# Two MLPs as one list of block products: weights two steps ahead, weight sums behind the reads of PSUM, first blocks fetched later

## The chip, the cores and the metric

The kernel runs on one core of one Trainium2 chip. The metric is the device time of one execution in microseconds (us). A profiled execution also gives the span from the first to the last instruction and the TensorE clock that was granted, 1.00 being full speed. Engines are named as in the profile: PE (TensorE matmul), PEld (its weight loads), DVE (VectorE), ACT (ScalarE), POOL (GpSimd), SP (the engine that here only issues DMAs).

## The reference

Two layers over 512 tokens of width 1024, all in float32. Layer 0 mixes by gated linear attention, layer 1 by stick-breaking attention; each mixer and each MLP is followed by a layer norm over a scaled residual.

```python
def sq_relu_mlp(x, w_up, w_down):            # x (512, 1024), w_up (1024, 4096), w_down (4096, 1024)
    h = jax.nn.relu(x @ w_up)
    return (h * h) @ w_down

# for each of the two layers
    h = layer_norm(DEEPNORM_ALPHA * h + mix, ln_g[layer, 0], ln_b[layer, 0])
    h = layer_norm(DEEPNORM_ALPHA * h + sq_relu_mlp(h, mlp_w_up[layer], mlp_w_down[layer]),
                   ln_g[layer, 1], ln_b[layer, 1])
```

DEEPNORM_ALPHA is the square root of 2 (`ALPHA` in the kernel). The mixers are not changed, but for the way in which two sums of weights of the layer-0 output projection are formed.

## The kernel before

**A float32 product is three matmuls.** Each float32 operand is cut into `hi` (its value rounded to fp32r) and `lo` (the rest), and a product is hi·hi + hi·lo + lo·hi. For weights, `split_tile` makes `hi` on ACT (L70) and `lo` on DVE (L72), each from a 128x1024 tile; `put` does the same for activations (L98 on ACT, L99 on DVE). Tags "hi" and "lo" have 8 buffers each, so four blocks of weights can stand ready.

**Products are Strassen-Winograd.** A matrix product of 2x2 blocks takes seven block products instead of eight, and sums of blocks before and after. `seven` does that for layer 0's output projection. In `mlp` the 4096 hidden columns are cut into four chunks c of 1024, and each chunk is an *up half* (`up(c)`: x times 1024 columns, 7 products of 48 matmuls of 128x256, L816) and a *down half* (`down(c)`: 1024 hidden values to the 1024 outputs, 7 products of 24 matmuls of 128x512, L909). The halves run as up(0), down(0), up(1), … down(3).

**Weights.** `Blocks` holds the blocks of one half: tag "B" has 8 buffers, four blocks in two tiles (h = 0, 1). The list `AHEAD` gives their order, (0,0), (1,0), (0,1), (1,1). SP loads each tile from HBM (L735). Where the table names a second block, POOL issues a DMA that adds it in flight (L737), so (0,1) becomes (0,1)+(0,0), and (1,1) becomes (1,1)+(0,1). Two further sums are made in place by `onto`: (0,0) += (1,1) and then (1,0) += (0,0), each on two tiles; on DVE (L761), or, for blocks listed in `by`, by a DMA that POOL issues from SBUF to SBUF (L759). The order of the seven products is p(0,0), p(1,0), p(0,1), p(0,0) after its sum, a plain block (1,1) loaded apart, p(1,1), p(1,0) after its sum. The page calls all these tiles B, whatever matrix they hold.

**Reading PSUM.** An up product fills two banks. A *fresh* read copies them on ACT (L824); a *closing* read adds or subtracts them on DVE (L830) and then takes relu and square on ACT (L831, L832); the last product of a half goes from PSUM straight through ACT (L883, L884). A down product is added to the residual rows `h` on DVE (L169, 128x512, or L167 the first time). PSUM has eight banks.

**Order.** The kernel is recorded in program order and a scheduler then places each engine's instructions; each engine runs its list strictly in that order. Instructions under `high_priority` are placed early, those passed through `keep` stay where the program has them. In the lists of before, a half's weight loads, splits and sums stand as early as their buffers allow.

**Start of an MLP.** The four 128-row tiles of `h` are normed one after another: `bn_stats` (L177), `bn_aggr` (L182) on DVE, `ve` and `rs` (L183, L184) on POOL, centring on DVE (L190), eight transposes per tile on PE (L261). Tiles 0 and 1 are turned before the first up product; those of tiles 2 and 3 are interleaved with the first two products (list `late`), from matmul step n = 8 of the first and n = 4 of the second. up(0) works on columns already split apart (`pieces_512`, or `ready` in layer 1). Its `Blocks` has `by` = (0,0), (1,0): four L759 DMAs in POOL's queue. The affine part of the norm (L196, per tile a product and a sum of two halves each) is done beside up(0) and down(0); the factor ALPHA of the residual sits in the first add (L167).

**End of an MLP.** down(3) has `by` = (0,0), (1,0) in both layers, so that all four sums are L759 DMAs. Its last three products are interleaved with the next norm.

## Time and profile before

| what | value |
| --- | --- |
| median of 3 runs | 1216.42 us (1211.41 to 1217.33) |
| the profiled execution | 1221.53 us |
| its span | 1219.8 us |
| mean granted TensorE clock | 0.949 |
| busy in that span | PE 1113.7, PEld 963.8, DVE 895.8, ACT 672.1, POOL 187.5 us |
| idle time of PE within the two MLPs and their starts | 18 gaps, 99.7 us |
| MLP of layer 0 | first up product's end of transposes 252.8 to 602.7 us |
| MLP of layer 1 | 864.5 to 1209.4 us |

The profiled execution is 5.11 us above the median and 1.73 us longer than its span. PE is busy 91% of the span, but a matmul at half clock counts as busy for twice as long, so the busy time holds the price of a low clock too. In a row of a timeline, a bracket at the end gives the idle time just before and what ended it. In a row of a table of windows stand the stretch, its length, then busy time and count for PE, PEld, DVE, ACT and POOL, the granted clock, the share of time for which the DMA engines were busy, and GB/s.

### The profile page before, as it was taken

The numbers are of one execution on the slowest core, as the hardware profiler recorded it, in microseconds if no ns is written. First come the engines' busy times: TensorE is split into PE (matmuls) and PEld (weight loads), VectorE is DVE, ScalarE is ACT, GpSimd is POOL, SyncE is SP. The second block draws the span as 40 slices with busy tenths as digits, with TensorE's granted clock in tenths as the row PEclk, the third lists the DMA queues.
The fourth block names the chain that finished last, engine by engine and source line by source line (L and its number), as shares of the span: only waits on it lengthen the run. The fifth ranks groups of instructions, "written<-read, shape, count | busy, mean of one in ns | idle before, by whom it ended". The sixth has DMA issues, their size and how long they took to land. (4 is left out here: it accounts for less than half of the span.)

```text
span 1219.8 us, 16750 instructions
## 1 busy us (share of the span) xinstructions
PE 1113.7 (91%) x6463; PEld 963.8 (79%) x6463; DVE 895.8 (73%) x1095; ACT 672.1 (55%) x963; POOL 187.5 (15%) x217
## 2 busy tenths in 40 slices
PE   9999998599978978998899999996999979979977
PEld 7888886597877877896788677785888868968965
DVE  4587467589758758686987887685898677677857
ACT  4464353585465455465674667755764644644743
POOL 1011220410110110111204001212021101101111
PEclk9999999799998998998999899997899979989989
DMA  7153696968866676677756216559478667667673
GB/s 218 53 172 87 187 237 150 245 184 188 223 166 176 145 191 174 151 195 170 211 114 191 88 63 128 121 148 232 141 190 211 182 164 183 178 171 170 198 182 69
DMA packets 125187, 202.77 MB, mean 166 GB/s; under 512 B 14202, under 2 KB 39162, under 8 KB 125108
## 3 DMA queue, kind: packets, MB, share of 16 engines
q1 hardware_dynamic: 92756, 131.97, 34.2%
q0 software_dynamic: 29888, 65.02, 29.7%
q10 hardware_dynamic: 2464, 4.72, 1.2%
q8 instruction: 51, 0.84, 0.3%
q14 instruction: 28, 0.23, 0.1%
HBM read 181.76 MB, written 3.15 MB: 152 GB/s over the span
## 5 line engine op out<-in xcount | busy, mean ns | idle before, releaser
L70 ACT ACTIVATE hi<-B 128x1024 fp32r<-128x1024 f32 x206 | 216.7, 1058 | 198.6 <-PE ps L909 38.9
L72 DVE TENSOR_TENSOR lo<-B,hi 128x1024 fp32r<-128x1024 f32 x206 | 247.6, 1221 | 87.8 <-ACT hi L70 87.6
L909 PE MATMUL ps<-hi,T 128*128 128x512 f32 x896 | 285.2, 398 | 15.7 <-ACT T L98 15.6
L816 PE MATMUL ps<-T,hi 128*128 128x256 f32 x1280 | 246.4, 295 | 45.8 <-DVE s L830 41.6
L816 PEld LDWEIGHTS ps<-T,hi 128*128 128x128 f32 x1280 | 211.3, 203 | 49.8 <-DVE s L830 43.4
L909 PEld LDWEIGHTS ps<-hi,T 128*128 128x128 f32 x896 | 171.4, 192 | 55.1 <-ACT T L98 17.3
L816 PE MATMUL ps<-T,lo 128*128 128x256 f32 x640 | 185.5, 293 | 0.0
L909 PE MATMUL ps<-lo,T 128*128 128x512 f32 x448 | 177.7, 398 | 0.0
L816 PEld LDWEIGHTS ps<-T,lo 128*128 128x128 f32 x640 | 129.0, 203 | 0.1
L70 ACT ACTIVATE hi<-raw 128x1024 fp32r<-128x1024 f32 x88 | 92.2, 1057 | 59.5 <-PE ps L94 15.0
L72 DVE TENSOR_TENSOR lo<-raw,hi 128x1024 fp32r<-128x1024 f32 x86 | 104.0, 1217 | 24.4 <-ACT hi L70 24.2
L909 PEld LDWEIGHTS ps<-lo,T 128*128 128x128 f32 x448 | 86.1, 192 | 17.8
L761 DVE TENSOR_TENSOR B<-B,B 128x1024 f32<-128x1024 f32 x36 | 43.2, 1222 | 77.2 <-DMA B<-in_mlp_w_down_dram 44.3
L816 PE MATMUL ps<-A,hi 128*128 128x256 f32 x512 | 93.0, 284 | 0.8 <-ACT s L824 0.6
L816 PEld LDWEIGHTS ps<-A,hi 128*128 128x128 f32 x512 | 79.8, 192 | 1.4 <-ACT s L824 1.4
L93 PE MATMUL ps<-T,hi 128*128 128x512 f32 (+1 forms) x200 | 80.1, 401 | 0.0
L737 POOL DMA_DIRECT2D B<-in_mlp_w_down_dram x32 | 38.7, 1210 | 258.5 <-DVE lo L72 189.8
L95 PE MATMUL ps<-T,lo 128*128 128x512 f32 (+1 forms) x200 | 76.6, 383 | 0.0
L94 PE MATMUL ps<-T,hi 128*128 128x512 f32 (+1 forms) x200 | 76.5, 382 | 0.0
L169 DVE TENSOR_TENSOR h<-h,ps 128x512 f32<-128x512 f32 x108 | 72.4, 680 | 2.2 <-PE ps L1254 1.5
L737 POOL DMA_DIRECT2D B<-in_mlp_w_up_dram x32 | 38.8, 1228 | 225.1 <-DMA B<-in_mlp_w_up_dram 136.8
L816 PE MATMUL ps<-A,lo 128*128 128x256 f32 x256 | 72.4, 283 | 0.0
(229 smaller groups left out, 1925.2 us busy)
## 6 DMA issues: line engine op xcount, KB each, us to landing
B<-in_mlp_w_up_dram SPq DMA_DIRECT2D x64, 512.0 KB, 4.4
B<-in_mlp_w_down_dram SPq DMA_DIRECT2D x64, 512.0 KB, 4.7
B<-in_mlp_w_up_dram POOLq DMA_DIRECT2D x32, 512.0 KB, 9.3
B<-in_mlp_w_down_dram POOLq DMA_DIRECT2D x32, 512.0 KB, 9.6
B<-B POOLq DMA_DIRECT2D x28, 512.0 KB, 5.2
raw<-in_mlp_w_up_dram SPq DMA_DIRECT2D x24, 512.0 KB, 4.9
raw<-in_gla_w_in_dram SPq DMA_DIRECT2D x20, 512.0 KB, 3.9
raw<-in_mlp_w_down_dram SPq DMA_DIRECT2D x16, 512.0 KB, 8.6
```

Source lines behind the costliest of these rows:

```text
L70: keep(nc.scalar.activation(hi, raw, AF.Copy))
L72: keep((on or nc.vector).tensor_tensor(lo, raw, hi.bitcast(F32), op=ALU.subtract))
L93: keep(nc.tensor.matmul(ps, lhsT=a[0], rhs=b[0], start=first, stop=False))
L94: keep(nc.tensor.matmul(ps, lhsT=a[0], rhs=b[1], start=False, stop=False))
L95: keep(nc.tensor.matmul(ps, lhsT=a[1], rhs=b[0], start=False, stop=last))
L169: nc.vector.tensor_tensor(h, h, ps, op=op)
L737: nc.gpsimd.dma_start(out=b.rearrange("p (a b) -> p a b", a=2), in_=weights(other[0], h, other[1]), accum_op=ALU.add)
L761: tt(x, x, y, op=ALU.add)
L816: nc.tensor.matmul(to, lhsT=b[k][x][:, fs], rhs=a(k)[:, y], start=opens and f % 2 == 0 and (k, x, y) == (0, 0, LO), stop=closes and (k, x) ...
L909: nc.tensor.matmul(banks[s], lhsT=a(k)[:, x][:, P * s:P * s + P], rhs=b[k][y], start=opens and (k, x, y) == (0, LO, 0), stop=closes and (k ...
```

## The change

1. **Steps.** up and down no longer run product by product: every block product becomes a `Step` with three parts, its weights (`blocks`), its activations (`operand`) and its matmuls and reads (`go`). All 56 steps of an MLP stand in one list `todo`, and `run_all` walks it: when it comes to step n it makes the weights of step n + 2 (and, from n = 6 on, that step's operand) and then issues step n.
2. **Sums behind.** `onto` now takes one half h, forms the sum and splits it at once, all four instructions held in program order by `keep`. It is called as the `blocks` of the two steps that use the sums, so two steps ahead and no earlier. DVE sums have line L767, DMA sums L765.
3. **Start.** up(0) keeps only (1,0) in `by`. Its `Blocks` loads (0,1) and (1,1) through SP as before; (0,0) and (1,0), four tiles, are loaded by POOL (L876) behind a copy of the last tile's `rs` (`pin`, L932). The late transposes in the first product move from n = 8 to m = 13 of its 16 places.
4. **Affine.** L196 is cut in two: `times` (a 128x1024 product, L199) beside up(0) and down(0), and `plus` (L202, with ALPHA) beside up(1).
5. **Output projection of layer 0.** `ends` is gone from `seven`: the sums of (1,1) and (2,1) blocks were formed by ten accumulating DMAs from HBM (L342) and are now four DMAs from SBUF to SBUF (L351).
6. One list of differences in the stick-breaking layer passes through `keep`.

```diff
-    def seven(a1, a2, weights, pool, hs, fresh, norms=(), mid=None, ends=False, begun=None):
+    def seven(a1, a2, weights, pool, hs, fresh, norms=(), mid=None, begun=None):
...
+        def onto(b, a):
+            nc.gpsimd.dma_start(out=b, in_=a, accum_op=ALU.add)
...
-            if ends:
-                more(b11, h, 0, 1)
-                more(b11, h, 1, 1)
-            else:
-                tt(b11, b22, b11, op=ALU.add)
+            onto(b11, b22)
...
-        def onto(self, a, b):
-            for x, y in zip(self.b[a], self.b[b]):
-                if a in self.by:
-                    nc.gpsimd.dma_start(out=x, in_=y, accum_op=ALU.add)
-                else:
-                    tt(x, x, y, op=ALU.add)
+        def onto(self, a, b, h):
+            x, y = self.b[a][h], self.b[b][h]
+            if a in self.by:
+                keep(nc.gpsimd.dma_start(out=x, in_=y, accum_op=ALU.add))
+            else:
+                keep(tt(x, x, y, op=ALU.add))
+            hi, lo = split_tile(x, 2, keep)
+            return [(hi[:, i, :], lo[:, i, :]) for i in range(2)]
...
+            table = (
+                (ys, True, False, (0, 0), True, blocks(0, 0, True)),
+                (xs, True, True, (0, 0), False, blocks(1, 0, True)),
+                (zs, True, False, (1, 1), True, blocks(0, 1)),
+                (ys, False, False, (0, 1), True, blocks(0, 0, sums=((0, 0), (1, 1)))),
+                (zs, False, True, (0, 1), False, blocks(2, 2)),
+                (ys, False, False, (1, 1), False, blocks(1, 1)),
+                (ys, False, True, (1, 0), None, blocks(1, 0, sums=((1, 0), (0, 0)))),
+            )
...
+                if after and n == 0:
+                    me.rest = lambda: (after(), made[0].load(AHEAD[:2], lambda **to: keep(nc.gpsimd.dma_start(**to))))
...
-                bs = Blocks(mlp_, w, AHEAD[2:] + AHEAD[:2], ((0, 0), (1, 0)))
...
+                    if c == 0 and late and (n == 0 and m == 13 and len(late) > 1 or n == 1 and m == 4):
+                        late.pop(0)()
...
+                def after():
+
+                    nc.gpsimd.tensor_copy(out=small(1, "pin"), in_=last)
+
+                made = steps(r[0], r[2], r[1], r[3], w, part, read, AHEAD[2:], ((1, 0),), plain, ops, after)
...
+        def run_all():
+            for n, step in enumerate(todo):
+                if n == len(todo) - 7:
+                    yield
+                for m in range(n, n + 3) if n == 0 else (n + 2,) if n > 5 else ():
+                    if m < len(todo):
+                        todo[m].make_blocks()
+                        if m > 6 or m < 2:
+                            todo[m].make_operand()
+
+                def between():
+                    if n == 0:
+                        step.rest()
+                    if n == 1:
+                        todo[2].make_operand()
+                    if 0 < n <= 5:
+                        todo[n + 2].make_operand()
+                        todo[n + 2].make_blocks()
+
+                yield from step.go(between)
```

Three places where the lists of instructions differ follow. B, lo, hi are weight tiles and their splits, ps a PSUM bank, s the up half's result, T an activation operand; numbers tell buffers apart and differ between the two programs.

The first is DVE at the passage from up(1) to down(1) in layer 0. Before, the sums of down(1)'s blocks (L761) stand ahead of up(1)'s closing reads of product 6 (L830, `ps516` and `ps517`):

```order
L830 TENSOR_TENSOR s2515_2915<-s2515_2915,ps529_3041 128x2x256
L761 TENSOR_TENSOR B548_3336<-B548_3336,B554_3350 128x1024
L72 TENSOR_TENSOR lo560_3365<-B549_3338,hi559_3363 128x1024
L761 TENSOR_TENSOR B549_3338<-B549_3338,B555_3353 128x1024
L830 TENSOR_TENSOR s2515_2915<-s2515_2915,ps516_2916 128x2x256
L99 TENSOR_TENSOR T563_3395<-s2515_2915,T563_3395 128x4x256
L830 TENSOR_TENSOR s2515_2915<-s2515_2915,ps517_2917 128x2x256
L72 TENSOR_TENSOR lo565_3400<-B550_3340,hi564_3398 128x1024
L72 TENSOR_TENSOR lo567_3404<-B551_3342,hi566_3402 128x1024
```

After, those reads carry line L915, and the first sum (L767) stands behind them and behind the first two adds of down(1) (L169):

```order
L915 TENSOR_TENSOR s2526_2965<-s2526_2965,ps523_2914 128x2x256
L72 TENSOR_TENSOR lo563_3305<-B551_3224,hi562_3303 128x1024
L915 TENSOR_TENSOR s2526_2965<-s2526_2965,ps524_2915 128x2x256
L72 TENSOR_TENSOR lo565_3309<-B552_3226,hi564_3307 128x1024
L99 TENSOR_TENSOR T566_3311<-s2526_2965,T566_3311 128x4x256
L72 TENSOR_TENSOR lo568_3368<-B553_3228,hi567_3366 128x1024
L72 TENSOR_TENSOR lo570_3372<-B554_3231,hi569_3370 128x1024
L830 TENSOR_TENSOR tmp571_3374<-s2526_2965,s2525_2964 128x1024
L169 TENSOR_TENSOR h304_1638<-h304_1638,ps573_3379 128x512
L99 TENSOR_TENSOR T572_3376<-tmp571_3374,T572_3376 128x4x256
L169 TENSOR_TENSOR h305_1639<-h305_1639,ps574_3393 128x512
L767 TENSOR_TENSOR B549_3220<-B549_3220,B555_3234 128x1024
```

So a wait of the sum for its transfers came ahead of reads that PE's last up product waits for, and now it comes behind them; the second sum of that block stands four rows further down.

The second is POOL at the start of layer 0's MLP. Before, the norms of tiles 2 and 3 (L183, L184) alternate with the sums by DMA (L759), each of which waits for transfers:

```order
L737 DMA B402_2082<-in_mlp_w_up_dram 128x2x512
L737 DMA B403_2085<-in_mlp_w_up_dram 128x2x512
L759 DMA B404_2088<-B402_2082 128x1024
L759 DMA B405_2090<-B403_2085 128x1024
L183 TENSOR_SCALAR ve382_2020<-mv381_2019 128x1
L184 TENSOR_TENSOR rs383_2021<-ve382_2020,mhalf_73 128x1
L759 DMA B406_2092<-B404_2088 128x1024
L759 DMA B407_2094<-B405_2090 128x1024
L183 TENSOR_SCALAR ve385_2041<-mv384_2040 128x1
L184 TENSOR_TENSOR rs386_2042<-ve385_2041,mhalf_73 128x1
```

After, they stand directly behind the loads, and the pinned copy and the plain loads come behind the last norm:

```order
L743 DMA B402_2076<-in_mlp_w_up_dram 128x2x512
L743 DMA B403_2079<-in_mlp_w_up_dram 128x2x512
L183 TENSOR_SCALAR ve382_2014<-mv381_2013 128x1
L184 TENSOR_TENSOR rs383_2015<-ve382_2014,mhalf_73 128x1
L183 TENSOR_SCALAR ve385_2035<-mv384_2034 128x1
L184 TENSOR_TENSOR rs386_2036<-ve385_2035,mhalf_73 128x1
L932 COPY pin412_2158<-rs386_2036 128x1
L876 DMA B413_2160<-in_mlp_w_up_dram 128x2x512
L876 DMA B414_2162<-in_mlp_w_up_dram 128x2x512
L876 DMA B415_2164<-in_mlp_w_up_dram 128x2x512
L876 DMA B416_2166<-in_mlp_w_up_dram 128x2x512
L765 DMA B415_2164<-B413_2160 128x1024
```

All four sums have left the norms' neighbourhood; two of them (L767) are now DVE's, the others (L765) come later in POOL's list.

The third is ACT at the passage into down(3) of layer 1. Before, the splits of the summed tiles (`hi785<-B752`, `hi787<-B753`) stand between the final reads of the up half and the operand `T777`:

```order
L70 ACTIVATE hi785_4993<-B752_4842 128x1024
L883 ACTIVATE s2710_4410<-ps712_4412 128x2x256
L884 ACTIVATE s2710_4410<-s2710_4410 128x2x256
L70 ACTIVATE hi787_4997<-B753_4844 128x1024
L883 ACTIVATE s2710_4410<-ps713_4413 128x2x256
L884 ACTIVATE s2710_4410<-s2710_4410 128x2x256
L98 ACTIVATE T777_4946<-tmp776_4944 128x4x256
```

After, the final reads come first, then the operand `T776`, then the splits of the first summed tiles (`B745`, `B746`):

```order
L912 ACTIVATE s2721_4464<-ps719_4414 128x2x256
L913 ACTIVATE s2721_4464<-s2721_4464 128x2x256
L912 ACTIVATE s2721_4464<-ps720_4415 128x2x256
L913 ACTIVATE s2721_4464<-s2721_4464 128x2x256
L98 ACTIVATE T776_4882<-tmp775_4880 128x4x256
L70 ACTIVATE hi779_4914<-B745_4716 128x1024
L70 ACTIVATE hi781_4919<-B746_4718 128x1024
```

The wait of a split for a sum by DMA came ahead of the last reads of the up half and of `T777`; now it comes behind both.

More of the change, by code (lines that the diff above doesn't have):

```diff
@@ L838, in other @@
+                if also and n >= (4 if c == 0 else 1):
                     also.pop(0)()
-            if c == 0:
-                ops[0], ops[1] = views([hT.a[0]]), views([hT.a[1]])
-            product(ops[0], p1, ys, True, False, (lambda n: n == 8 and len(late) > 1 and late.pop(0)()) if c == 0 else None)
-            fresh(ys, 0, 0)
+                return ()
+            r = [lambda u=u, s=s: hT.r[u][:, :, s] for u in range(2) for s in (LO, HI)]
             if c:
-                p2 = bs.pieces(1, 0)
@@ L885, in up @@
-            return a1, a2
-        def down(c, a1, a2, norms=(), by=(), also=()):
+                made = steps(*(None,) * 4, w, part, read, AHEAD, ops=ops)
+            else:
+                plain = [ready[:4], ready[4:]] if ready else [pieces_512(mlp_w_up[l], 512 * k, 4, 0) for k in range(2)]
+                last = hs[3].rs
+                def after():
+                    nc.gpsimd.tensor_copy(out=small(1, "pin"), in_=last)
+                made = steps(r[0], r[2], r[1], r[3], w, part, read, AHEAD[2:], ((1, 0),), plain, ops, after)
@@ L888, in down @@
+            return made, [lambda s=s, j=j: sq[j][:, :, s] for j in range(2) for s in (LO, HI)]
+        def down(c, q, norms=(), by=(), also=()):
             w = lambda k, h, j: block(mlp_w_down[l], 1024 * c + 512 * k + 256 * h, 512 * j)
-            a11, a21, a12, a22 = a1[:, :, LO], a1[:, :, HI], a2[:, :, LO], a2[:, :, HI]
-            bs = Blocks(mlp_, w, AHEAD, by)
-            ys, xs, zs = ([None, None] for _ in range(3))
             seen = set()
             also = list(also)
-            def other():
-                if also:
-                    also.pop(0)()
@@ L913, in product @@
-            def product(a, b, banks, opens, closes, i, j, last=False):
-                for s in range(2):
-                    part(s, a, b, banks, opens, closes)
-                    add(s, banks, i, j, last)
-            first = operand(a11)
-            product(first, bs.pieces(0, 0), ys, True, False, 0, 0)
-            second = operand(a12), bs.pieces(1, 0)
-            other()
-            product(*second, xs, True, True, 0, 0, last=True)
-            t = temp()
-            tt(t, a22, a21, op=ALU.subtract)
@@ L925, in down @@
-            third = operand(t), bs.pieces(0, 1)
-            other()
-            bs.onto((0, 0), (1, 1))
-            product(*third, zs, True, False, 1, 1)
-            minus(t, t, a11)
-            bs.onto((1, 0), (0, 0))
-            fourth = operand(t), bs.pieces(0, 0)
-            product(*fourth, ys, False, False, 0, 1)
-            minus(a12, a12, t)
-            p3 = operand(a12), bs.plain(1, 1)
-            tt(a11, a11, a21, op=ALU.subtract)
-            p7 = operand(a11), bs.pieces(1, 1)
@@ L951, in mlp, with part @@
-        keep = tc.keep_in_program_order
-        turns = [lambda h=h: h.affine(vec, keep) for h in hs]
-        for c in range(NC - 1):
-            a1, a2 = up(c, turns[:2] if c == 0 else ())
-            for _ in down(c, a1, a2, by=((1, 0),), also=turns[2:] if c == 0 else ()):
-                pass
-        a1, a2 = up(NC - 1)
-        steps = down(NC - 1, a1, a2, norms=range(NT) if l == 0 else (2, 3), by=((0, 0), (1, 0)))
-        got = done(steps, four, mlp_)
+            def part(a, b, banks, opens, closes, n):
+                for s in range(2):
+                    if opens:
+                        banks[s] = bank()
+                    for k in range(4):
+                        for x, y in ((LO, 0), (LO, 1), (HI, 0)):
+                            nc.tensor.matmul(banks[s], lhsT=a(k)[:, x][:, P * s:P * s + P], rhs=b[k][y],
+                                             start=opens and (k, x, y) == (0, LO, 0),
+                                             stop=closes and (k, x) == (3, HI), skip_group_check=True)
+                    yield s
@@ new lines, in read @@
+            def read(s, banks, i, j, first, n):
+                last = not first and 2 * i + s in norms
+                hs[2 * i + s].add(j, banks[s], c == 0 and (i, j, s) not in seen, last, ALU.subtract if j else ALU.add)
+                seen.add((i, j, s))
+                if also and s == 1 and n < 2:
+                    also.pop(0)()
+                if norms and n > 3:
+                    yield (s, ~s, 2 + s)[n - 4]
+            return steps(q[0], q[2], q[1], q[3], w, part, read, AHEAD, by)
@@ L960, in mlp @@
+        every = run_all()
+        next(every)
+        got = done(every, four, mlp_)
         ml.__exit__(None, None, None)
@@ L1313, in yoco_kernel @@
             if p == 1:
-                differences(1)()
+                differences(1)(keep)
         if p == NP - 1:
```

203 lines of the change are left out of this document (100 added, 103 removed).

## The prediction, made before the changed kernel was run

> **What bounds the kernel now.** I read the page first, then PE's and DVE's waits, then windows laid around PE's long gaps, and last the timelines at these places. From the page, engine totals and one group:
>
> ```profile
> PE 1113.7 (91%) x6463; PEld 963.8 (79%) x6463; DVE 895.8 (73%) x1095; ACT 672.1 (55%) x963; POOL 187.5 (15%) x217
> L761 DVE TENSOR_TENSOR B<-B,B 128x1024 f32<-128x1024 f32 x36 | 43.2, 1222 | 77.2 <-DMA B<-in_mlp_w_down_dram 44.3
> ```
>
> PE is the bound by its average, but no engine is full. The DVE sums cost 43.2 us of work and 77.2 us of waiting ahead of them. The waits of PE (us in total, times, longest), then those of DVE and POOL:
>
> ```profile
> PE ps L816 <- DVE s L830: 41.6, 4, 11.0
> PE ps L261 <- DVE h L190: 21.4, 5, 10.5
> PE ps L909 <- ACT T L98: 15.6, 4, 6.6
> PE ps L261 <- DVE mv L182: 11.5, 2, 8.1
> DVE B L761 <- DMA B<-in_mlp_w_down_dram: 44.3, 8, 11.6
> DVE h L190 <- POOL rs L184: 27.8, 12, 11.8
> ```
>
> Four waits of PE for a closing read (L830) make 41.6 us, and eight waits of DVE for down weights make 44.3. One of the four shows that they are the same thing. DVE first, then PE, after up(1) of layer 0:
>
> ```profile
> 352.92 1.28 DVE L830 TENSOR_TENSOR s<-s,ps 128x512 f32<-128x512 f32 x2
> 365.36 1.23 DVE L761 TENSOR_TENSOR B<-B,B 128x1024 f32<-128x1024 f32 x1 [11.16 <-DMA B<-in_mlp_w_down_dram]
> 367.90 1.23 DVE L761 TENSOR_TENSOR B<-B,B 128x1024 f32<-128x1024 f32 x1 [0.18 <-DMA B<-in_mlp_w_down_dram]
> 369.04 0.68 DVE L830 TENSOR_TENSOR s<-s,ps 128x512 f32<-128x512 f32 x1
> 369.78 0.58 PE L816 MATMUL ps<-T,hi 128*128 128x256 f32 x1 [10.74 <-DVE s L830]
> ```
>
> The read that PE needs stands behind two sums of weights for the next half, which wait until 365.36 and 367.90 for their transfers. What this costs per half is read from windows that end where PE's products of a half end. The first, third, fourth and fifth are the four up halves with the stall, the second is a down half and the sixth an up half without one, the seventh is down(3) of layer 1, the eighth and ninth are the two starts, and the last is 3.4 us after a short gap:
>
> ```profile
> 324.85:378.23 53.38, 42.45 (x330) 42.04 (x329) 31.82 (x31) 27.34 (x31) 7.85 (x7) 0.87 0.69 161
> 378.23:416.33 38.10, 38.10 (x170) 31.53 (x169) 32.52 (x34) 21.09 (x22) 4.83 (x4) 1.00 0.78 210
> 416.33:470.47 54.14, 43.10 (x337) 42.90 (x336) 31.89 (x31) 26.35 (x30) 6.61 (x6) 0.87 0.63 144
> 939.14:992.64 53.50, 42.42 (x329) 42.01 (x328) 31.83 (x31) 27.31 (x31) 7.81 (x7) 0.87 0.69 162
> 1030.75:1082.15 51.40, 42.56 (x337) 42.35 (x336) 31.89 (x31) 26.64 (x30) 7.02 (x7) 0.90 0.63 149
> 1120.26:1160.94 40.68, 40.68 (x338) 40.48 (x337) 29.44 (x29) 25.61 (x29) 5.85 (x5) 1.00 0.70 185
> 1160.94:1207.49 46.55, 39.90 (x162) 31.57 (x161) 31.39 (x38) 21.39 (x27) 4.92 (x7) 0.89 0.44 107
> 207.70:252.82 45.12, 25.13 (x157) 23.31 (x157) 27.48 (x38) 25.68 (x50) 12.72 (x16) 0.81 0.89 219
> 829.25:864.48 35.23, 22.15 (x135) 20.49 (x135) 20.23 (x26) 20.61 (x40) 8.15 (x11) 0.80 0.84 228
> 300.60:304.00 3.40, 3.40 (x10) 2.58 (x9) 3.40 (x4) 2.66 (x4) 0.00 (x0) 0.50 1.00 217
> ```
>
> A quiet up half takes 40.68 us and a quiet down half 38.10, both with PE busy throughout at clock 1.00. Those are the floors.
>
> **The change, part by part.**
>
> *A. Sums behind the closing reads.* The excess of the four stalled halves is 53.38 + 54.14 + 53.50 + 51.40 − 4 × 40.68 = 49.7 us. Idle time and the half clock that follows it are both in that. In the new order the reads come ahead of the sums, so this wait goes. What is late next is the sum itself. Before, its two transfers had landed 40.5 and 43.1 us after the half began (365.36 and 367.90 against 324.85). The new places are behind the first two adds of the down half, about 40.7 + 5.4 (a seventh of 38.10) = 46.1 us, and some 4 us further down. Buffers come free a few microseconds later too, since the sums and splits that read them move back, so the slack is between 0 and about 6 us. I keep 2 us per half, 1 of idle time and 1 of clock, and take 49.7 − 8 = 41.7. The bounds are 0 (the stall keeps its size under another name) and 49.7.
>
> DVE is the cover, and it is thin in a down half. By the order, a down half after the change has 14 `lo` splits, 2 sums, 7 operand splits and 4 differences, 27 instructions of 128x1024, and 14 adds of 128x512. Back to back they take what the chain shows in down(3):
>
> ```profile
> 1187.07 1.14 DVE T L99
> 1188.21 0.59 DVE h L169
> ```
>
> 27 × 1.14 + 14 × 0.59 = 39.0 us against 38.10 of PE. Over a pair of halves the sum is what DVE does now, 31.82 + 32.52 = 64.3 us in 40.68 + 38.10 = 78.8. The excess of 0.9 fits in the two steps of lead (2 × 5.4 us), which the up half rebuilds, so I cost it at nothing. Without that lead it is 6 × 0.9 = 5.4 us.
>
> *B. Splits behind the last reads in down(3).* PE waited there on an operand that stood behind the split of a summed tile. ACT, PE, and the two sums in POOL's queue, layer 1:
>
> ```profile
> 1173.79 1.06 ACT L70 ACTIVATE hi<-B 128x1024 fp32r<-128x1024 f32 x1 [11.10 <-DMA B<-B]
> 1178.39 0.79 PE L909 MATMUL ps<-hi,T 128*128 128x512 f32 x1 [6.61 <-ACT T L98]
> 1163.92 0.90 POOL L759 DMA_DIRECT2D B<-B  x1 [4.68 <-DMA B<-in_mlp_w_down_dram]
> 1166.51 0.86 POOL L759 DMA_DIRECT2D B<-B  x1 [1.69 <-DMA out_dram<-lnb]
> ```
>
> This half's excess is 46.55 − 38.10 = 8.45 us. Layer 0 has the smaller one. L909's four waits are 15.6 in all: 6.61 here, 2.14 and 1.86 at the two down(0) (E below), which leaves 4.99, and by proportion 4.99 × 8.45 / 6.61 = 6.4 us of excess. After the change the operand goes first, and the split is wanted only by the fourth product, 3 × 5.44 = 16.3 us into the half. The second sum was issued 5.6 us into it and, at the first one's 9.8 us (1163.92 to about 1173.7), lands at 15.4. With buffers free 3 to 4 us later it is about 3 us late in layer 1, 5 with the clock. In layer 0 I keep 1. Saved: 3.4 + 5.4, rounded down to 8.4. Bounds 0 and 14.8.
>
> *C. Start of layer 0's MLP.* Two waits of PE, the POOL and DVE rows behind the second:
>
> ```profile
> 215.77 1.52 PE L261 MATMUL ps<-ident,h 128*128 128x128 f32 x6 [8.07 <-DVE mv L182]
> 238.44 1.97 PE L261 MATMUL ps<-ident,h 128*128 128x128 f32 x8 [10.51 <-DVE h L190]
> 233.42 0.90 POOL L759 DMA_DIRECT2D B<-B  x1 [12.78 <-DMA B<-in_mlp_w_up_dram]
> 235.73 0.86 POOL L759 DMA_DIRECT2D B<-B  x1 [1.42 <-DMA B<-in_mlp_w_up_dram]
> 207.59 1.06 ACT L70 ACTIVATE hi<-B 128x1024 fp32r<-128x1024 f32 x1 [12.44 <-DMA B<-in_gla_w_o_dram]
> ```
>
> The norm of tile 2 stood in POOL's queue behind two sums that waited for transfers, and its L190 behind that. The new order has L183 and L184 ahead of every sum, so 10.51 goes. The other wait, 8.07, is for statistics that stand on DVE behind the split of output-projection weights whose DMA sum landed at 207.5. These ten accumulations from HBM become four from SBUF, issued for the same tiles; medians on the page:
>
> ```profile
> B<-in_mlp_w_down_dram POOLq DMA_DIRECT2D x32, 512.0 KB, 9.6
> B<-B POOLq DMA_DIRECT2D x28, 512.0 KB, 5.2
> ```
>
> Up to three accumulations in a row at 9.6 become one at 5.2, so this wait goes too. In full clock the stretch holds 25.13 × 0.81 = 20.4 us of PE work; with 3.1 for an operand gap of E's size below and its clock it lasts 23.5 and saves 21.6. Against that, two sums that POOL did (L759) are now DVE's, with their splits, ahead of the third product's reads: 4 × 1.14 = 4.6 us if nothing covers them, 0 if all is covered; I take 3.1 (and 1 of clock), because up(0) has little DVE slack while it also splits its own operands. Net 17.5; bounds 0 and 24.7.
>
> The four plain loads cross to POOL's queue and wait there for the last `rs`. Four issues at L759's 0.90 and a landing like its 5.2 end some 9 us after that norm; the sums that use them are formed two products later (2 × 40.68 / 7 = 11.6 us), so I cost them at nothing; uncovered, they cost one landing, 5.2 us. The pinned copy and the transposes' later place cost what a POOL row of 0.6 and 16 small matmuls cost anyway: 0.
>
> The Trainium skill ("DMA: Bandwidth & Descriptors", section "SWDGE vs HWDGE vs iDMA") speaks against this move: plain transfers belong on SP or ACT, and GpSimd is for accumulation. If that price falls on the path in both layers, the sum is 2 × 5.2 us worse, 1153; the rows above put it behind cover, and I go by them.
>
> *D. Start of layer 1's MLP.* The same reordering, with less to win:
>
> ```profile
> 834.58 0.90 POOL L759 DMA_DIRECT2D B<-B  x1 [0.82 <-DMA B<-in_mlp_w_up_dram]
> 837.33 0.90 PE L261 MATMUL ps<-ident,h 128*128 128x128 f32 x3 [8.08 <-DVE h L190]
> ```
>
> L759 goes, but POOL still issues its accumulations behind SP's loads ahead of this norm. L759's part is 0.82 + 0.90 = 1.7 ahead of this tile and as much ahead of the next, each with 1.7 of clock (E): 6.8 in all, less 3.1 as in C and rounded down: 3.5. Bounds −3 and 17.5 (35.23 − 22.15 × 0.80).
>
> *E. down(0) and the affine.* The first products of down(0) in the two layers:
>
> ```profile
> 300.23 0.93 PE L909 MATMUL ps<-hi,T 128*128 128x512 f32 x2 [2.14 <-ACT T L98]
> 914.29 0.74 PE L909 MATMUL ps<-hi,T 128*128 128x512 f32 x2 [1.86 <-ACT T L98]
> ```
>
> PE waits there beside L196's rows, half of which move to up(1). Each such gap also had a half-clock stretch of 3.40 us behind it (last window), so 1.7 more: 7.4 in both layers. I take 2; bounds −2 and 7.4.
>
> On that clock the Trainium skill ("TensorE: Matmul & The Clock Gate", Part 1) has the throttle return after an idle window of about 3.4 us and asks only for no gap above that. Here a gap of 2.14 us was followed by 3.40 us at 0.50, so the trace differs and I charge clock to short gaps. By the page the leftover gaps would cost no clock, and the sum would be about 6 us better, 1137.
>
> **The sum.** 41.7 + 8.4 + 17.5 + 3.5 + 2 = 73.1. The profiled 1221.53 becomes 1148.4; it stood 5.1 above the median of 1216.42, so against that median I expect 1143.
>
> **Rivals.**
>
> *R1, the transfers become the bound.* The same bytes move in less time. A pair of halves moved with share 0.69 × 53.38 + 0.78 × 38.10 = 66.5 us of full DMA time; in 78.8 that is 0.84, and up to 0.89 and 1.00 are seen in the windows above. If the last accumulated blocks are then late in each of the six pairs by 3 us with 1.7 of clock, it is 28 us: 1171. For it: the slack of 0 to 6 us in A. Against it: the share stays below 0.89.
>
> *R2, everything closes.* All upper bounds, 49.7 + 14.8 + 24.7 + 6.7 + 7.4 = 103.3, give 1113. Against it: the slack of DVE and of the sums.
>
> *R3, slower.* Splits for step n + 2 stand on DVE and ACT ahead of the reads of earlier steps; one tile that is late then holds the queue at each step, where before it held one product per pair. It decides at 73 / 56 = 1.3 us per product in all 56 of them; at 1.8 the time is 1244. For it: 39.0 against 38.1 in down halves. Against it: in the quiet halves the same splits stand as far ahead, with no gap.
>
> *R4, the stall only changes its name.* The sum's wait meets the adds of the down half and A saves nothing: 1143 + 41.7 = 1185. Against it: transfers that land at 43.1 for a place at 46.1.
>
> **How the numbers follow.** Forecast 0.73, R1 0.12, R2 0.06, R4 0.04, R3 0.03, no net change 0.02. The forecast's own range is 1125 to 1163. From R2's upper part to R1's and the start of R4's, 1117 to 1178 leaves out about 0.18. About 0.5% (6 us) can be told from no change: faster 0.94, same 0.02, slower 0.04 (R3 and a part of the unforeseen).
>
> **What would show it.** A: the up halves c = 1, 2 at 41 to 43 us, clock 1.00, no wait of PE for a closing read above 2 us; the sums' line waits less than 20 us in all. B: down(3) below 44 us. C: 207.70 to the end of the last transposes near 27, no L190 wait for POOL above 3 us. D: 32. The prediction is wrong if PE waits on weights (`hi`, `lo`) at the third or seventh step of each half (R1), on adds (R4), or if small gaps stand at most steps (R3).

## The result, and the profile after

The median is 1130.13 us (1128.15 to 1137.22) against 1216.88: ratio 0.931 (0.926 to 0.936), 86.8 us faster. The profiled execution took 1129.37 us with a span of 1127.6. The forecast of 1143 was 13 us too slow, within its range. Between the two profiled executions the spans differ by 92.2 us, because the one before stood 5.1 us above its median and the one after 0.8 us below.

Engine totals, the granted clock in 40 slices, and the group of DVE sums after the change, from the page (the group from the view by lines):

```profile
PE 1091.5 (97%) x6463; PEld 942.9 (84%) x6463; DVE 898.9 (80%) x1083; ACT 669.8 (59%) x963; POOL 182.8 (16%) x217
PEclk9999999999999999999999999998999999999989
L767 DVE TENSOR_TENSOR B<-B,B 128x1024 f32<-128x1024 f32 x40 | 48.8, 1219 | 1.0 <-DMA B<-in_mlp_w_up_dram 1.0
```

PE's idle time in the whole span fell by 70.0 us, from 106.1 to 36.1. (Within the two MLPs and their starts the 18 gaps of before add up to 94.1 us, not 99.7.) PE has the same 6463 matmuls, but 22 us less busy time, since fewer of them ran at half clock. The sums are four more than before, 40 for 36, and DVE waits 1.0 us ahead of them where it waited 77.2. The longest waits of PE, in the same columns as those of before:

```profile
PE ps L948 <- ACT T L98: 8.1, 4, 3.5
PE ps L267 <- DVE h L190: 8.0, 3, 5.8
PE ps L899 <- DVE lo L72: 3.7, 4, 1.5
PE ps L948 <- DVE h L169: 2.1, 1, 2.1
```

The wait of 41.6 us for closing reads is gone, that for statistics (11.5) too, and the other two of before are 8 us each. Where the time came from shows in windows whose bounds are the same points of the program in both kernels: the end of the output projection's uninterrupted products, of down(0), of down(2), of down(3), and the same in layer 1. Before:

```profile
207.70:325.01 117.31, 95.19 (x572) 85.41 (x573) 97.90 (x116) 70.29 (x99) 22.97 (x25) 0.91 0.79 199
325.01:508.74 183.73, 161.77 (x1003) 148.03 (x1002) 128.61 (x130) 95.89 (x103) 22.90 (x20) 0.93 0.70 175
508.74:602.69 93.95, 85.07 (x522) 75.94 (x521) 70.31 (x78) 55.04 (x72) 14.46 (x15) 0.95 0.72 174
602.69:829.25 226.56, 223.94 (x1260) 177.99 (x1259) 178.32 (x260) 143.40 (x273) 37.03 (x47) 0.98 0.52 132
829.25:939.31 110.06, 95.06 (x550) 84.99 (x551) 90.66 (x104) 64.36 (x89) 18.41 (x20) 0.89 0.72 189
939.31:1120.42 181.11, 161.19 (x1002) 147.46 (x1002) 128.60 (x130) 96.15 (x103) 23.22 (x21) 0.93 0.71 178
1120.42:1209.36 88.94, 82.29 (x505) 73.42 (x505) 62.66 (x69) 48.08 (x56) 11.17 (x12) 0.94 0.56 141
```

After:

```profile
207.67:307.20 99.53, 94.07 (x588) 83.02 (x589) 88.20 (x97) 67.12 (x96) 23.28 (x27) 1.00 0.87 221
307.20:463.50 156.30, 156.30 (x1001) 142.65 (x1001) 133.24 (x135) 94.45 (x102) 23.07 (x21) 1.00 0.79 203
463.50:550.96 87.46, 82.91 (x507) 73.83 (x506) 66.78 (x75) 50.84 (x68) 13.14 (x16) 0.96 0.71 174
550.96:771.53 220.57, 219.74 (x1260) 176.29 (x1259) 181.36 (x262) 146.62 (x277) 36.27 (x46) 1.00 0.55 138
771.53:873.82 102.29, 91.41 (x566) 81.32 (x567) 88.22 (x95) 65.39 (x90) 19.97 (x23) 0.97 0.77 202
873.82:1031.22 157.40, 156.65 (x1001) 142.68 (x1001) 133.14 (x135) 94.34 (x102) 23.51 (x21) 1.00 0.79 202
1031.22:1118.58 87.36, 81.71 (x491) 72.68 (x490) 63.90 (x70) 48.05 (x56) 13.06 (x14) 0.94 0.56 143
```

In the two middle pairs of each layer PE is now busy throughout at clock 1.00, but for one wait of 0.74 us in layer 1. After the change more matmuls of the next up half stand ahead of the last product of a down half than before: 16 more at the end of down(0), which are 1.9 us, and 15 more at the end of down(2), 1.8 us. Moved back to their own stage, the savings against the terms forecast are:

| stage | saved, us | forecast |
| --- | --- | --- |
| chunks 1 and 2 (A) | 27.4 + 23.7 − 2 × (1.9 − 1.8) = 50.9 | 41.7 |
| chunk 3 (B) | 6.5 + 1.6 − 2 × 1.8 = 4.5 | 8.4 |
| start and chunk 0, layer 0 (C, half of E) | 17.8 + 1.9 = 19.7 | 18.5 |
| start and chunk 0, layer 1 (D, half of E) | 7.8 + 1.9 = 9.7 | 4.5 |
| between the MLPs | 6.0 | 0 |
| after the last product | 1.4 | 0 |

Together they are 92.2, the difference of the spans (1219.8 − 1127.6).

### The profile page after: what moved, and what is told of

Same layout as the page of the kernel before. It is cut to its first block, busy times and chain, and to the rows that moved or that the text cites. A ratio compares the mean times of both kernels' runs of the same rounds, so it can differ in the third digit from the quotient of the medians.

```text
span 1127.6 us, 16741 instructions
## 1 busy us (share of the span) xinstructions
PE 1091.5 (97%) x6463; PEld 942.9 (84%) x6463; DVE 898.9 (80%) x1083; ACT 669.8 (59%) x963; POOL 182.8 (16%) x217
## 5 line engine op out<-in xcount | busy, mean ns | idle before, releaser
L70 ACT ACTIVATE hi<-B 128x1024 fp32r<-128x1024 f32 x206 | 213.5, 1054 | 158.5 <-DVE B L767 65.6
L948 PE MATMUL ps<-hi,T 128*128 128x512 f32 x896 | 286.4, 397 | 11.5 <-ACT T L98 8.1
L899 PE MATMUL ps<-T,hi 128*128 128x256 f32 x1280 | 233.0, 284 | 4.4 <-DVE T L99 2.0
L948 PEld LDWEIGHTS ps<-hi,T 128*128 128x128 f32 x896 | 170.7, 191 | 52.6 <-ACT T L98 10.2
L899 PEld LDWEIGHTS ps<-T,hi 128*128 128x128 f32 x1280 | 199.5, 192 | 8.2 <-ACT T L98 2.7
L899 PE MATMUL ps<-T,lo 128*128 128x256 f32 x640 | 179.7, 284 | 3.7 <-DVE lo L72 3.7
L899 PEld LDWEIGHTS ps<-T,lo 128*128 128x128 f32 x640 | 121.9, 192 | 5.0 <-DVE lo L72 4.8
L948 PEld LDWEIGHTS ps<-lo,T 128*128 128x128 f32 x448 | 85.7, 191 | 17.8 <-DVE lo L72 0.7
L98 ACT ACTIVATE T<-s 128x1024 fp32r<-128x1024 f32 (+1 forms) x52 | 51.5, 993 | 53.2 <-DVE s L842 37.0
L169 DVE TENSOR_TENSOR h<-h,ps 128x512 f32<-128x512 f32 x108 | 71.4, 680 | 4.2 <-PE ps L948 3.5
```

Source lines behind the costliest of these rows:

```text
L70: keep(nc.scalar.activation(hi, raw, AF.Copy))
L98: keep(nc.scalar.activation(hi, ps, AF.Copy))
L169: nc.vector.tensor_tensor(h, h, ps, op=op)
L899: nc.tensor.matmul(to, lhsT=b[k][x][:, fs], rhs=a(k)[:, y], start=opens and f % 2 == 0 and (k, x, y) == (0, 0, LO), stop=closes and (k, x) ...
L948: nc.tensor.matmul(banks[s], lhsT=a(k)[:, x][:, P * s:P * s + P], rhs=b[k][y], start=opens and (k, x, y) == (0, LO, 0), stop=closes and (k ...
```

## The experiments

The kernel after was timed in one group of runs, with the median of 1130.13 us above, while the kernel before was timed in every group and had medians between 1216.42 and 1220.3. So a difference of about 3 us or less against 1130 says little by itself.

**The sums alone, in the kernel before.**

```diff
-                    tt(x, x, y, op=ALU.add)
+                    tc.keep_in_program_order(tt(x, x, y, op=ALU.add))
```

> The kernel before with one change: the DVE sums of weights (L761) are held in program order, so that in the lists they stand behind the closing reads of the up half and beside the first adds of the down half, as after the change; steps, lead, start, affine and output projection stay as before. Theory 1 (the place of the sums behind the reads is the whole of A): the four stalled up halves fall from 51.4 to 54.1 us to 41 to 42, about 48 us come off, near 1168 us. Rival (the lead of two steps and the splits made with the sums are needed as well): the wait moves into the down halves, less than 25 us come off, above 1190 us.

Measured: 1166.29 us against 1217.56 for the kernel before, ratio 0.957 (0.955 to 0.960), 51 us. Chunks 1 and 2 of both layers:

```profile
327.26:487.44 160.18, 157.42 (x1002) 142.97 (x1002) 129.12 (x132) 94.43 (x103) 22.86 (x20) 1.00 0.79 200
908.56:1065.80 157.24, 156.84 (x1002) 142.80 (x1002) 129.06 (x132) 94.41 (x103) 22.85 (x20) 1.00 0.80 204
```

They take 160.2 and 157.2 us where they took 183.7 and 181.1; with the same bounds they take 156.4 and 157.5 after the change. One word on one line, and with it the place of 36 instructions in DVE's list, is 47.4 of A's 50.9 us. The 3.5 us that are left sit in layer 0.

**The sums not held, in the kernel after.**

```diff
-                keep(tt(x, x, y, op=ALU.add))
-            hi, lo = split_tile(x, 2, keep)
+                tt(x, x, y, op=ALU.add)
+            hi, lo = split_tile(x, 2)
```

> The kernel after with keep taken off the DVE sum and its split, the program's order unchanged. In the lists the sums then stand behind the last closing reads but ahead of the first add of the down half, about 5 us earlier than after the change. Theory 1 (what counts is that the closing reads come first): pairs of halves stay within 2 us of after, 1130 to 1136. Rival R4 (a wait of the sums for their transfers just meets the next reads, the adds): 4 pairs with 3 to 6 us more, 1142 to 1154.

Measured: 1200.79 us (1196.37 to 1207.61). R4 was too small: 71 us go. Chunks 1 and 2 take 184.0 and 186.1 us in the two layers, 56 more together, and the first chunks 14 more. The edit did not do what the expectation took for granted, that the sums stay behind the closing reads. In down(2) of both layers a sum stands ahead of such a read (L915) again, as in the kernel before. Layer 0:

```profile
443.43 1.23 DVE L767 TENSOR_TENSOR B<-B,B 128x1024 f32<-128x1024 f32 x1 [6.34 <-DMA B<-in_mlp_w_down_dram]
448.22 0.68 DVE L915 TENSOR_TENSOR s<-s,ps 128x512 f32<-128x512 f32 x1
448.95 0.79 PE L899 MATMUL ps<-T,hi 128*128 128x256 f32 x2 [6.83 <-DVE s L915]
```

The sums for up(2) and up(3) stand ahead of an add of the down half before. Layer 0, and the matmul that waits for that add:

```profile
400.17 1.23 DVE L767 TENSOR_TENSOR B<-B,B 128x1024 f32<-128x1024 f32 x1 [7.52 <-DMA B<-in_mlp_w_up_dram]
401.31 0.68 DVE L169 TENSOR_TENSOR h<-h,ps 128x512 f32<-128x512 f32 x1
402.05 0.80 PE L948 MATMUL ps<-hi,T 128*128 128x512 f32 x1 [6.29 <-DVE h L169]
```

The scheduler, left free, moved the sums some 15 to 17 us forward, ahead of reads that PE needs; each sum waited for its transfer, and PE for the read: 14.2 us in two waits for closing reads and 22.3 us in six for adds. Only in down(1) does the sum come behind the closing reads and ahead of the first add; there it waited 5.2 us, and PE lost 0.5. So this run does not refute theory 1, since its condition did not hold. It shows that the place has to be held. In the change itself the sum finds its data. DVE in down(1) of layer 0 after the change, no wait in the row of the sum:

```profile
350.80 0.68 DVE L169 TENSOR_TENSOR h<-h,ps 128x512 f32<-128x512 f32 x1
351.40 1.22 DVE L767 TENSOR_TENSOR B<-B,B 128x1024 f32<-128x1024 f32 x1
```

By the trace, the transfers had landed at 347.5 and 352.0 for sums that began at 351.4 and 355.4: a margin of 3.9 and 3.4 us. It is not as wide everywhere. In layer 0 it was 0.2 and 2.2 us in up(2), 4.7 and 0.6 in down(2), 1.0 and 2.4 in up(3).

**One step of lead.**

```diff
-                for m in range(n, n + 3) if n == 0 else (n + 2,) if n > 5 else ():
+                for m in range(n, n + 3) if n == 0 else (7,) if n == 6 else () if n < 6 else (n + 1,):
```

> The kernel after with weights and operands made one step ahead instead of two (from the seventh step on). Theory 1 (the lead is the cover for the sums: two sums, four splits on ACT and DVE are 6 to 7 us in a row, longer than a step of 5.4 to 5.8): PE waits 1 to 3 us in steps 4 and 7 of 15 halves, 30 to 60 us with the clock, 1160 to 1190. Rival (only the place behind the reads counts, and sums made later meet their transfers less): within 5 us of 1130.

Measured: 1200.37 us (1199.11 to 1202.01), 70 us more and above what Theory 1 gave. The window of chunks 1 and 2 of layer 0, then PE's longest waits:

```profile
309.73:482.16 172.43, 162.49 (x1010) 142.71 (x1010) 133.56 (x134) 92.23 (x102) 22.82 (x20) 1.00 0.72 184
```

```profile
PE ps L948 <- ACT T L98: 22.9, 13, 8.8
PE ps L948 <- ACT hi L70: 15.5, 3, 7.7
```

A pair is about 8 us longer, in many waits of 2.6 us at the most, and PE's clock stays at 1.00. The long ones, up to 8.8 us, are in down(3), where the sums come by DMA: chunk 3 takes 18.5 and 18.9 us more. The lead is a condition of the result, as theory 1 had it, though the time lies above the 1160 to 1190 us given there. The edit takes the lead from the activations' operands as well as from the weights, and no run tells the two apart.

**The output projection's accumulations.**

```diff
-            onto(b11, b22)
+            more(b11, h, 0, 1)
+            more(b11, h, 1, 1)
...
-            onto(b21, b11)
+            for k, j in ((0, 0), (0, 1), (1, 1)):
+                more(b21, h, k, j)
```

> The kernel after with the two sums of layer 0's output projection formed again by ten accumulating DMAs from HBM in place of four from SBUF. Theory (C, first wait): the 8.07 us wait of the first transposes at 207.6 returns, with about 2 to 3 of half clock, and the start of layer 0's MLP (23.9 us after the change) becomes 32 to 35; time 1139 to 1141. Rival (this wait came from the order of DVE, which the other edits changed too): start unchanged, 1130.

Measured: 1139.75 us (1137.11 to 1141.34), 9.6 more. The wait is back, at the same transposes:

```profile
215.54 0.87 PE L267 MATMUL ps<-ident,h 128*128 128x128 f32 x3 [8.49 <-DVE mv L182]
```

**Start of the MLPs as before.**

```diff
-                made = steps(..., AHEAD[2:], ((1, 0),), plain, ops, after)
+                made = steps(..., AHEAD[2:] + AHEAD[:2], ((0, 0), (1, 0)), plain, ops, after)
...
-                    me.rest = lambda: (after(), made[0].load(...))
+                    me.rest = lambda: None
```

> The kernel after with up(0)'s blocks loaded as before: all four blocks by SP up front, both sums by DMA in POOL's queue, no pinned copy. Theory (C, second wait, and D): the norm of tile 2 stands again behind sums that wait for transfers; the start of layer 0 goes from 23.9 to about 36 us and that of layer 1 from 26.7 to about 29; against that the wait of 1.5 + 0.4 us in the third product after the start goes in both layers. Net +9 to +12, 1139 to 1142. Rival (the plain loads on POOL and the DVE sums cost as much as they save): within 3 us of 1130.

Measured: 1136.71 us (1135.99 to 1141.49), 6.6 more. POOL, then PE:

```profile
225.27 0.89 POOL L765 DMA_DIRECT2D B<-B  x1 [12.85 <-DMA B<-in_mlp_w_up_dram]
228.75 0.57 POOL L184 TENSOR_TENSOR rs<-ve,mhalf 128x1 f32<-128x1 f32 x1
230.22 1.12 PE L267 MATMUL ps<-ident,h 128*128 128x128 f32 x4 [9.20 <-DVE h L190]
```

In layer 0 the wait returns with 9.2 us. The sum is less than forecast because in layer 1 the two forms come out even: from the end of layer 0's MLP to the end of layer 1's down(0) it takes 323.1 us (559.51 to 882.57) in this run and 322.9 (550.96 to 873.82) after the change. That is a gain and a loss of about the same size. Layer 1's start with the old form, then after the change:

```profile
779.85:810.26 30.41, 19.93 (x135) 18.47 (x135) 17.94 (x24) 18.06 (x38) 8.16 (x11) 0.89 0.85 221
771.53:798.22 26.69, 19.43 (x134) 18.25 (x135) 17.94 (x24) 17.97 (x38) 8.00 (x12) 0.87 0.54 149
```

The start itself is 3.7 us shorter in the new form, and the products from there to the end of down(0) are 3.3 us longer: 75.6 us after the change, 72.3 in this run, in layer 0 as in layer 1. The two sums that are DVE's in the new form are formed there.

**The affine as before.**

```diff
-        turns = [lambda h=h: h.times(vec, keep) for h in hs]
+        turns = [lambda h=h: h.affine(vec, keep) for h in hs]
...
-            made, q = up(c, turns[:2] if c == 0 else plus if c == 1 else ())
+            made, q = up(c, turns[:2] if c == 0 else ())
```

> The kernel after with the affine of the norm done whole beside up(0) and down(0) again (L196, four half-wide rows per tile), nothing of it in up(1). Theory (E: that work on DVE makes the wait at down(0)): the first chunk of each layer gets 2 to 4 us longer, the second 0 to 1 shorter; time 1133 to 1137. Rival (DVE has room there, the gain at down(0) came from steps and lead): within 2 us of 1130.

Measured: 1136.98 us (1135.37 to 1142.09), 6.9 more by the medians and 5.6 by the profiled spans, 3.0 and 2.6 of them in the first chunk of each layer. At down(0):

```profile
288.88 0.50 PE L948 MATMUL ps<-hi,T 128*128 128x512 f32 x1 [3.77 <-ACT T L98]
859.68 0.67 PE L948 MATMUL ps<-hi,T 128*128 128x512 f32 x1 [3.79 <-ACT T L98]
```

The same waits are 1.48 us after the change. So E is confirmed, and worth 5.6 us where the sum had 2.

**The transposes' place.**

```diff
-                    if c == 0 and late and (n == 0 and m == 13 and len(late) > 1 or n == 1 and m == 4):
+                    if c == 0 and late and (n == 0 and m == 8 and len(late) > 1 or n == 1 and m == 4):
```

> The kernel after with the transposes of tile 2 at the ninth place of the first product again, not the fourteenth. Theory (with the norms no longer held in POOL's queue the tile is ready by then in layer 0, but in layer 1 its norm comes later): layer 0 within 1 us, layer 1 a wait of 1 to 3 us at these transposes, time 1130 to 1134. Rival (the later place is worth the waits that it was put there for): 5 us or more in either layer, 1136 and up.

Measured: 1128.83 us (1127.45 to 1131.06), no difference that can be told. The later place brings nothing.

**The subtractions in the stick-breaking layer**, both ways: `differences(1)(keep)` in the kernel before, and `differences(1)()` in the one after.

> The kernel before with one change: the subtractions of the value differences in the stick-breaking layer pass through keep. Theory: the stretch between the MLP of layer 0 and the start of layer 1's norm, 213.2 us before and 207.5 after, falls to 207.5 on this word alone; the time falls by 5.7 us to about 1211. Rival: those 5.7 us came from the MLP (buffers or transfers that come free earlier), and nothing changes: 1216.9.

> The kernel after with the keep on the value differences taken out again. Theory: the stretch between the two MLPs goes from 207.5 back to 213.2 us, time 1135.8. Rival (the gain came from elsewhere): 1130, the stretch stays at 207.5.

Measured: alone 1216.29 us against 1217.56 (ratio 0.997, 0.9945 to 0.9998), its profiled span 5.2 us shorter; undone 1133.5 (1131.39 to 1134.52), 3.4 more, its span 2.0 longer. Where the mixer's matmuls are compared one by one, the gain and the loss sit at one place, 6.0 us in the one run and 4.0 in the other, and 5.8 of the 6.0 us that the change saves between the MLPs sit there too. At that place the kernel before has two waits of the score products (L1159), and the slow clock behind them in the windows that follow:

```profile
676.82 1.78 PE L1159 MATMUL ps<-k,q 64*128 64x512 f32 x17 [0.88 <-DVE q L1148]
679.65 1.55 PE L1159 MATMUL ps<-k,q 64*128 64x256 f32 x6 [1.06 <-ACT wt L1198]
```

```profile
679.00:682.00 3.00, 2.35 (x8) 1.28 (x10) 2.77 (x4) 3.00 (x9) 0.00 (x0) 0.58 0.17 48
682.00:686.00 4.00, 4.00 (x17) 1.83 (x14) 3.65 (x7) 2.33 (x6) 0.00 (x0) 0.50 0.97 283
```

Without keep, four subtractions of 0.6 us stand ahead of a query read (L1148) in DVE's list; with it they come behind. The two waits are 1.9 us, and most of the rest is half clock behind them. In the run of the sums alone, which has no keep here either, one wait of 1.05 us was left, the clock stayed at 1.00 and the place took about 3 us less than before. So what the word is worth depends on whether the clock falls. The theory's place is right; of its 5.7 us the medians confirm 1 to 3.

**More transfers.**

```diff
                     if other:
+                        x = self.pool.tile([P, 512], F32, tag="x", bufs=1, name=nm("x"))
+                        nc.sync.dma_start(out=x, in_=self.w(k, h, j)[:, 0, :])
```

> The kernel after with four extra loads of 256 KB in each half, issued by SP behind the loads of the blocks that are accumulated, into a tile that nothing reads: about 14% more bytes from HBM in an MLP. The DMA share of a pair of halves, 0.79 to 0.80 after the change, would come to about 0.9. Theory (transfers have room): a pair gets 0 to 2 us longer, 1130 to 1142. Rival R1 (transfers are next to the bound; sums that land late hold DVE's queue): 4 us or more in each of six pairs, 1155 and up.

Measured: 1180.73 us (1175.27 to 1181.48). It doesn't settle R1. The extra loads wait for nothing but each other, so the scheduler placed all 32 of a layer in its first two chunks, about a fifth more bytes there (8.4 MB on 37.7) and none later. In layer 0, 27 of them were issued before 329 us, ahead of the first window below, which holds the other five. Chunks 1 and 2 of layer 0:

```profile
329.44:416.17 86.73, 81.80 (x493) 74.46 (x493) 69.03 (x70) 47.87 (x52) 13.47 (x12) 0.94 0.86 221
416.17:495.34 79.17, 79.17 (x510) 72.24 (x510) 64.43 (x66) 47.17 (x51) 11.36 (x11) 1.00 0.78 199
```

The pair with the five is 9.6 us longer (77.14 after the change) at a share of 0.86, and SP waited 7.6 and 10.2 us at the longest for one extra load before the next. Whether bytes or SP's queue make the loss stays open.

**A last sum on DVE, and what is better still.**

```diff
-            todo += down(c, q, ..., ((0, 0), (1, 0)) if ends else ((1, 0),),
+            todo += down(c, q, ..., ((1, 0),),
```

> The kernel after with the first sum of down(3) formed on DVE, as in the other down halves, instead of by DMA. In layer 1 that DMA was issued 5.3 us into the half and landed at 13.7 and 16.9; ACT's split waits for it with the next operand behind. Theory (B's rest is the sum's transfer): the waits of 3.5 us in layer 1 and 1.6 + 0.5 + 0.5 in layer 0 go, with the half clock behind them: 6 us in layer 1, 2 to 3 in layer 0, time 1121 to 1123. Rival (DVE has no room in that half, where norms come in): nothing gained or up to 5 us lost, 1130 to 1135.

Measured: 1122.55 us (1121.73 to 1123.53), 7.6 less. ACT in down(3) of layer 1 after the change, and then the window of chunk 3 of that layer with this edit:

```profile
1083.28 1.06 ACT L70 ACTIVATE hi<-B 128x1024 fp32r<-128x1024 f32 x1 [7.88 <-DMA B<-B]
```

```profile
1030.18:1107.46 77.28, 77.22 (x490) 69.89 (x490) 63.45 (x69) 46.80 (x55) 9.55 (x9) 1.00 0.55 145
```

It takes 77.3 us where it took 87.4, without a wait. Chunk 3 of the two layers saves 14.0 us together. Some 7.0 of them come back: 3.5 at the start of layer 1's mixer and 3.5 behind the last product, as waits and half clock. To this I added a second edit for layer 1's start, where a wait of 5.85 us was left: POOL issues an accumulation at 774.26 after 7.54 us of waiting for its load, and the norm of tile 1 stands behind it.

```diff
-                    if other:
-                        nc.gpsimd.dma_start(..., accum_op=ALU.add)
+                    if other and not (self.hold and k):
+                        self.more(b, h, other)
...
-                    me.rest = lambda: (after(), made[0].load(...))
+                    me.rest = lambda: (after(), [keep(made[0].more(b, h, (0, 1))) for h, b in enumerate(made[0].b[1, 1]) if l], made[0].load(...))
```

> The kernel after with two edits: the first sum of down(3) on DVE (as measured, 1122.6), and in layer 1 the two accumulations of block (1,1) of up(0) issued behind the pinned copy, so that the norm of tile 1 no longer stands in POOL's queue behind an accumulation that waits for its load (rs came 5.6 us late). Theory: the wait of 5.6 us of the transposes at layer 1's start and 2 us of clock go, 1115 to 1117. Rival (the accumulation, 13 us later, makes the sum late for the fourth product): the gain comes back as a wait there, 1120 to 1125.

Measured: 1117.9 us (1116.07 to 1119.84), ratio to the kernel before 0.917 (0.914 to 0.920), the fastest version. POOL at that place:

```profile
771.66 0.22 POOL L183 TENSOR_SCALAR ve<-mv 128x1 f32<-128x1 f32 x1 [3.44 <-DVE mv L182]
```

It now waits for the statistics alone. The first up matmul of layer 1 comes 7.4 us sooner after the end of layer 0's MLP, a part of it clock in the mixer; from there to the end of down(0) the layer got 3.6 us longer (94.5 for 90.9), with waits of 1.3 and 1.6 us of up products for splits. So the wait goes, as the theory had it, and about half of the gain comes back later, as the rival had it.

## Why the prediction was right, and where its sizes were off

By the spans the sum was 19 us too low, 73.1 for 92.2: A gave 9.2 us more than forecast, D 5.2 and C 1.2 (each with half of E), and 7.4 came from places that the sum does not have; B gave 3.9 less. The total is near because A, the largest term, was read rightly, and not because errors cancelled.

**A** was read rightly: one wait, twice written, and its price from windows against a quiet half (49.7). The term was sized too low, 41.7 for 50.9, chiefly by the 2 us per half kept for sums that come late. They waited 1.0 us in all 40. The pairs came out even a little below the floor: the four together take 313.7 us, where eight quiet halves would take 315.1, so 49.7 was no bound. My slack of 0 to 6 us was 0.2 to 4.7 in layer 0; and it is there only because the sums are held, with 71 us at stake, so R4, at 0.04, was nearer than its chance said.

**B** failed in size, 8.4 for 4.5: in layer 0 4.7 for 5.4, in layer 1 −0.2 for 3.4. The late sum was there as the step had it. It landed 16.9 us into the half (1086.52 against 1069.59), and PE waited 3.5 us with 4.4 us at half clock behind it, 5.7 in all for the 5 that I kept. What the step missed is the other end of the half: PE's last product waited 2.1 us for an add that stood in DVE's list behind pieces of the norm, with the clock at 0.78 in the 7.6 us after it. That took 3.8 us more. The half had also been priced too short: its window ended at 1207.49, 1.9 us ahead of its last product (1209.36 in the table above), so its excess before was 10.3 us and not 8.45. After the change down(3) took 48.9 and 49.0 us in the two layers, where the step has 39 to 43. With the first sum on DVE both waits went, so the second hung on the first.

**C** held: 19.7 with half of E for 18.5, and both waits came back one by one when their cause was put back (9.6 and 6.6 us). The plain loads moved to POOL cost nothing that shows in layer 0: the sums that use them began without a wait. The charge of 4.1 for DVE's two new sums was about right: the products behind the start are 3.3 us longer in the new form, with waits for `lo` of 1.5 + 0.4 us in the fourth product.

**D** was sized too low, with its half of E 4.5 for 9.7. Of PE's wait of 8.08, 5.85 stayed, as the row of POOL's queue had said; the start of the MLP still became 26.7 us from 35.2. Of these 8.5 us the new order of the start, the cause that I had named, is worth 3.7, by the run with the old one, and the products behind it give 3.3 back. The other 4.8 us, 2.6 less idle time and 2.2 less half clock, came with other parts of the change; which of them, no run shows. E adds 2.6 in the products behind the start.

**E** was sized 2 and measured 5.6.

**Not in the sum at all:** 6.0 us between the MLPs, and 1.4 after the last product. I costed the `keep` on the value differences by not mentioning it. 5.8 of the 6.0 sit at its place, as waits and half clock; by the medians it is worth 1 to 3 us.

R2's sum of all upper bounds took 6.7 for D, whose own bound was 17.5. With half of E it measured 9.7.

**The clock.** I charged 1 to 1.7 us of it to every leftover gap. That is not how it goes: behind gaps of 1.48 us the clock stayed at 1.00, behind one of 1.47 us in the fastest version it fell, and the last section shows what decides it. The Trainium skill ("TensorE: Matmul & The Clock Gate", Part 1) has the throttle return after an idle window of about 3.4 us. The traces agree on the length of the window and differ in that it need not be idle throughout; 1.9 us of it were enough.

R1 and R3 did not occur: the share of 0.79 in the pairs is below the 0.84 forecast for them, and no gap above 0.8 us stands in chunks 1 and 2.

## What to carry to other kernels

When a wait of PE names a vector read, look at what stands ahead of that read in the same engine's list: an instruction for the next stage that waits for a transfer costs there what it would cost nowhere else. Put it behind the reads that PE needs next and ahead of its use by more than its own length, and hold it there, since a scheduler that was free to move it put it some 16 us forward, and 71 of the 87 us were lost. Then look for the same shape on the other in-order queues; here ACT's splits behind a DMA sum and POOL's norm behind an accumulation were 12 us more, by the fastest version against the kernel after.

## What was not expected of the hardware

The length of a wait does not tell whether the granted clock falls behind it. Two stretches of the kernel after and the same two of the fastest version, with a wait of PE of 1.48 us that ends at 239.79 in the one and of 1.47 us that ends at 241.99 in the other:

```profile
238.57:241.99 3.42, 2.20 (x18) 2.20 (x19) 3.42 (x4) 1.09 (x2) 0.82 (x1) 1.00 0.63 120
241.99:245.40 3.41, 3.06 (x25) 2.86 (x25) 3.41 (x5) 3.41 (x6) 0.06 (x1) 1.00 0.80 205
238.57:241.99 3.42, 1.75 (x14) 1.34 (x12) 3.42 (x4) 1.63 (x3) 0.96 (x1) 1.00 0.52 101
241.99:245.40 3.41, 3.41 (x16) 3.41 (x17) 3.41 (x4) 2.30 (x4) 0.88 (x1) 0.50 0.36 76
```

The bounds of these stretches are steps of the clock itself. In the 14 traces of this case the granted clock changes 212 times, and within each trace all changes lie on one grid of 3.413 us; a stretch at half clock lasts one to four whole steps. What goes with a fall is PE's idle time within one step of the grid. In the kernel after it is 3.42 − 2.20 = 1.2 us, since the wait begins in the step before; in the fastest version the wait lies within one step, which has 1.7 us idle, and the next step is at 0.50.

Two longer waits show the same, 3.23 us up to 541.22 in the run with the transposes' earlier place and 3.22 us up to 550.09 in the run with the start of before:

```profile
536.30:539.72 3.42, 1.69 (x8) 1.07 (x6) 3.42 (x8) 0.00 (x0) 0.29 (x2) 1.00 0.78 281
539.72:543.13 3.41, 1.91 (x14) 1.77 (x15) 3.06 (x6) 1.25 (x4) 3.33 (x5) 1.00 0.00 0
546.04:549.45 3.41, 0.82 (x4) 0.36 (x2) 3.06 (x8) 0.00 (x0) 1.07 (x4) 1.00 0.55 208
549.45:552.86 3.41, 2.77 (x11) 2.61 (x12) 2.94 (x4) 1.64 (x5) 3.41 (x3) 0.50 0.16 10
```

The first is cut in two by the bound of a step, 1.7 and 1.5 us idle, and the clock stays at 1.00 in the second stretch and in the step after it; the second puts 2.6 us into one step, and the next is at 0.50. Over all traces, every step at clock 1.00 with more than 1.9 us idle was followed by 0.50, and only one with less than 1.5 (1.23) was; between 1.5 and 1.9 both occur. All 58 waits of 3.4 us or more in the 14 traces were followed by half clock; of the shorter ones some were and some were not, by where they fell on the grid, and where the grid lies against the program differs from trace to trace. Why the clock goes by this grid, no run shows. Two waits of 0.88 and 1.06 us of which 1.6 us fell into one step (L1159 in the kernel before) were also followed by 0.50, and a stage with many short waits that are spread over the steps (one step of lead) kept the clock at 1.00.
